# Start of a transformer block on one Trainium2 core: loads shared between two queues, x turned in pieces, sums joined at the end of a step

## The chip, the cores and the metric

The kernel runs on one core of a Trainium2 chip. The core has a matrix engine (PE, with its weight loads shown as PEld), a vector engine (DVE), a scalar engine (ACT), a general engine (POOL, also called GpSimd) and a queue engine that only starts transfers (SP). SP and POOL can both start DMAs; all of them run on the same 16 DMA engines. Each engine works through its own list in order, and waits on semaphores for the others. The metric is the device time of one execution in microseconds (us), as the median of several runs.

## What is computed

One transformer block on 512 tokens of width 2048: six modulation vectors from a conditioning vector c, a normed and modulated input h, a wide projection of h by `w_in`, a convolution mixer and a sparse attention mixer on the parts of the projection, an output projection, and a gated feed-forward network. The part that matters here is the beginning:

```python
sh_a, sc_a, g_a, sh_f, sc_f, g_f = jnp.split(jax.nn.silu(c) @ ada_w[l] + ada_b[l], 6, axis=-1)
h = modulate(rms_norm(x, norm_mix[l]), sh_a, sc_a)      # h * (1 + scale) + shift
proj = h @ w_in[l]
cb, cc, ch, q, kc, vc, ksl, vsl, kw, vw, gl = jnp.split(proj, splits, axis=-1)
...
```

All numbers are float32. x is 512 x 2048 (4.2 MB); the two modulation vectors that h needs take the first 4096 columns of `ada_w` (2048 rows each, 33.6 MB); three blocks of 512 columns of `w_in` are multiplied in this first stage (12.6 MB).

## The kernel before

The first stage runs from the start of the program to about 213 us; the rest of the block follows it with the matrix engine busy nearly all the time. The stage goes over the 2048 rows of `w_in` in eight **column steps** of 256 rows (two chunks of 128, `STEP` = 2). Before a column step can run, its 256 entries of shift and scale must be there, and each of them is a sum over all 2048 rows of `ada_w`. So there are also eight **sum steps** (`start_steps`), one for each column step. A sum step loads its 512 columns of `ada_w` as eight tiles of 512 KB, two transfers of 256 KB each. A tile holds two of the 16 row chunks. DVE multiplies each chunk by its entry of silu(c) and adds it to an accumulator `acc` (line 347 in the kernel before, 128 x 512 elements an instruction). From the second sum step on, the first four chunks are done by PE (`SHARE` = 4, line 341), and DVE's first instruction reads PE's result from PSUM as its addend. PE then adds up the 128 partitions (`column_sums`, line 224), and DVE makes the entries `mod` from it (lines 356 to 359).

x is loaded as four tiles of 1 MB; ACT squares and sums their halves (line 384), DVE scales the identity by the norms (`dg`, line 388), and PE turns and scales x in one product, 16 chunks times four tiles (line 413), which ACT copies to `xnT` (line 415).

A column step (`start_columns`) makes h of its two chunks on ACT from `xnT` and `mod`, split into a high part and a low part (lines 436, 439), then multiplies one block of `w_in` (`CKC`) into four PSUM tiles that stay open over all steps (lines 457 to 460), and, where a group of steps ends, blocks of two more column ranges (`CKS`, `CQ`) token by token (lines 115 to 117 through `mm3`), added to `ksv` and `q0` by DVE (line 495). Each block of `w_in` is also split into a high part on ACT (line 107) and a low part on DVE (line 109). float32 products are three such part products.

What sets the order: every engine's list is made once, when the program is built, from the order of the code and from explicit hints (`tc.issue_after(latest[...])`, not ahead of a noted instruction). `weave` lets the sum steps of later columns (the iterator `ahead`) run between the pieces of a column step, so many yields for each column step. All transfers of this stage are started by SP, in one list. A transfer also waits until the buffer that it writes is free: the `ada_w` tiles and the blocks of `CKS` and `CQ` share a ring of 8 buffers of 512 KB (`aring`), the blocks of `CKC` have a ring of 4 (`ring[0]`).

Of the kernel before, what the change touches and what calls it, by code (L numbers as in the profile page):

```python
# [72 lines left out]
def block_kernel(ctx: ExitStack, tc: tile.TileContext, a: dict, out: bass.AP):  # L73
# [83 lines left out]
    nc.scalar.activation(cT, cT, AF.Silu)  # L157
    xts = []
# [5 lines left out]

    const = cp.tile([P, CONST_W], F32, name="const")
    nc.sync.dma_start(const, a["shape_const"][:, :CONST_W])
    fold = sp.tile([P, 32], F32, name="fold")
    nc.sync.dma_start(fold, a["shape_const"][:, CONST_W:])
# [143 lines left out]
    aring = pool("araw", 8, stack=st0)  # L312
# [7 lines left out]
    def start_steps(k0):  # L320
# [6 lines left out]
        by_array = range(SHARE if k0 else 0)  # L327
        raws, pr = [], aux() if k0 else None
        for ka in range(0, KC, 2):
# [3 lines left out]
            for k in range(ka, ka + 2):  # L333
                w, s = raw[:, k - ka, :], cT[:, k:k + 1]
                if k in by_array:
# [3 lines left out]
                    with tc.issue_after(latest["columns"]):  # L339
                        for j, v in enumerate(raws):  # L340
                            nc.tensor.matmul(pr[32 * j:32 * j + 32, :], cz[:, k - 3 + j, :], v, start=k < 4,
                                             stop=k + 1 == SHARE, skip_group_check=True)
                    raws = []
                elif k == 0:
                    nc.vector.tensor_scalar(acc, w, s, None, op0=ALU.mult)
                else:
                    nc.vector.scalar_tensor_tensor(acc, w, s, pr if k == SHARE and k0 else acc, op0=ALU.mult, op1=ALU.add)
            yield
        if k0:
            yield  # L350
            yield
        with tc.issue_after(latest["columns"]):
# [6 lines left out]
        nc.vector.scalar_tensor_tensor(d[:, 1, :], d[:, 1, :], 1.0, g, op0=ALU.add, op1=ALU.mult)  # L359

# [4 lines left out]
    for name, n in ROWS.items():  # L365
        src = a[name].rearrange("l (k p) -> (l k) p", p=P) if name != "conv_w" else \
            a[name][0].rearrange("t (k p) -> (t k) p", p=P)
        nc.sync.dma_start(vrow[r0:r0 + n, :], src)
        at[name] = r0
        r0 += n  # L370
    nc.sync.dma_start(brow, a["ada_b"].rearrange("l (k p) -> (l k) p", p=P))
    for dst, src, n in ((cols, vrow, nrow), (bcol, brow, NB6)):
        ps = aux()
        nc.tensor.transpose(ps[:, :n], src, ident[:n, :n])
        nc.vector.tensor_copy(dst, ps[:, :n])

    dgs = []
    for i in range(NT):
# [3 lines left out]
        for m in range(2):  # L382
            junk = sp.tile([P, D // 2], F32, tag="junk", name="junk")
            nc.scalar.activation(junk, xt[:, m * D // 2:(m + 1) * D // 2], AF.Square, accum_out=sh[:, m:m + 1])
# [5 lines left out]
    for _ in range(4):  # L390
# [1183 lines left out]
```

## Time and profile before

| | us |
|---|---|
| runs of before: median (lowest to highest) | 2210.16 (2205.81 to 2211.21) |
| the profiled execution, whole | 2208.49 |
| its span in the trace | 2206.7 |
| PE busy in the span | 2141.2 (97%) |
| DVE busy | 1777.8 (81%) |
| ACT busy | 1077.9 (49%) |

The span leaves 1.8 us of the execution outside. The page's slices show where PE isn't full: the first two or three of 40 (each 55 us), and hardly anywhere else. DMA share, in the tables below, is the mean busy share of the 16 DMA engines, and the number behind it what they moved in GB/s. In the timeline a row has the start, the duration, the engine, the line and the operation, and in brackets how long the engine was idle before it and who ended that.

### The profile page before, as it was taken

The numbers are of one execution on the slowest core, as the hardware profiler recorded it, in microseconds if no ns is written. First come the engines' busy times: TensorE is split into PE (matmuls) and PEld (weight loads), VectorE is DVE, ScalarE is ACT, GpSimd is POOL, SyncE is SP. The second block draws the span as 40 slices with busy tenths as digits, with TensorE's granted clock in tenths as the row PEclk, the third lists the DMA queues.
The fourth block names the chain that finished last, engine by engine and source line by source line (L and its number), as shares of the span: only waits on it lengthen the run. The fifth ranks groups of instructions, "written<-read, shape, count | busy, mean of one in ns | idle before, by whom it ended". The sixth has DMA issues, their size and how long they took to land.

```text
span 2206.7 us, 30495 instructions
## 1 busy us (share of the span) xinstructions
PE 2141.2 (97%) x10981; PEld 1789.7 (81%) x10981; DVE 1777.8 (81%) x2762; ACT 1077.9 (49%) x1807; POOL 220.9 (10%) x284
## 2 busy tenths in 40 slices
PE   5899999999999898999999999999999999999998
PEld 4578778878878686888888888888888878888887
DVE  4787968878878697698888888888888876878787
ACT  5334434554543554745555555555554455545443
POOL 0000000000000223001110110100110021212132
PEclk9999999999999999999999999999999999999999
DMA  8993776545558978456666565666665499998897
GB/s 287 305 304 115 245 249 182 182 140 149 157 166 247 243 169 180 115 181 173 173 159 174 160 165 155 169 170 168 161 174 146 161 260 256 208 232 199 226 182 181
DMA packets 387932, 422.89 MB, mean 192 GB/s; under 512 B 21952, under 2 KB 293700, under 8 KB 387012
## 3 DMA queue, kind: packets, MB, share of 16 engines
q1 hardware_dynamic: 352388, 318.15, 46.2%
q0 software_dynamic: 35392, 102.79, 23.6%
q8 instruction: 86, 1.41, 0.3%
q14 instruction: 66, 0.54, 0.1%
HBM read 385.20 MB, written 19.94 MB: 184 GB/s over the span
## 4 chain that ended last, share of the span: by engine, by line
PE 88%; DMA 6%; DVE 2%; issue 1%; ACT 1%; POOL 1%; SPq 0%; ACTq 0%; POOLq 0%; DVEq 0%
PE main L1270 15%; PE aux L1270 11%; PE aux L1046 11%; PE main L1046 10%; PE main L1272 8%; PE aux L1272 6%; PE main L115 5%; PE main L117 5%; PE main L116 5%; DMA t<-in_w_out 2%; PE aux L861 2%; DMA y<-in_x 2%; PE aux L833 2%; PE aux L115 1%; PE aux L116 1%
## 5 line engine op out<-in xcount | busy, mean ns | idle before, releaser
L1270 PE MATMUL main<-hC,whi 128*128 128x512 f32 x1408 | 355.4, 394 | 0.0
L1270 PEld LDWEIGHTS main<-hC,whi 128*128 128x128 f32 x1408 | 253.8, 189 | 46.0 <-DVE hC L1137 0.5
L1270 PE MATMUL aux<-hC,whi 128*128 128x512 f32 x1072 | 268.8, 392 | 0.0
L1270 PEld LDWEIGHTS aux<-hC,whi 128*128 128x128 f32 x1072 | 192.8, 189 | 34.0
L1263 DVE TENSOR_TENSOR wlo<-xy,whi 128x1024 fp32r<-128x1024 f32 x135 | 164.6, 1219 | 62.6 <-ACT whi L1257 62.6
L1257 ACT CAST whi<-xy 128x1024 fp32r<-128x1024 f32 x135 | 141.4, 1048 | 147.2 <-PE main L1270 78.0
L1272 PEld LDWEIGHTS main<-hC,wlo 128*128 128x128 f32 x1408 | 192.3, 190 | 14.3
L1272 PE MATMUL main<-hC,wlo 128*128 128x256 f32 x1408 | 196.2, 282 | 0.0
L1046 PE MATMUL main<-wlo,phi 128*128 128x512 f32 x420 | 166.6, 398 | 13.1 <-DVE wlo L998 7.4
L1046 PE MATMUL aux<-wlo,phi 128*128 128x512 f32 x420 | 164.2, 391 | 1.8 <-DVE wlo L998 1.8
L1046 PE MATMUL main<-whi,phi 128*128 128x512 f32 x420 | 165.9, 395 | 0.0
L1046 PE MATMUL main<-whi,plo 128*128 128x512 f32 x420 | 165.7, 395 | 0.0
L1046 PE MATMUL aux<-whi,phi 128*128 128x512 f32 x420 | 163.5, 389 | 0.0
L1046 PE MATMUL aux<-whi,plo 128*128 128x512 f32 x420 | 163.5, 389 | 0.0
L115 PE MATMUL main<-alo,whi 128*128 128x512 f32 x384 | 155.7, 406 | 0.0
L1272 PEld LDWEIGHTS aux<-hC,wlo 128*128 128x128 f32 x1072 | 146.3, 190 | 10.5
L996 ACT CAST whi<-xy 128x1024 fp32r<-128x1024 f32 x88 | 92.8, 1055 | 120.3 <-PE main L1046 58.4
L117 PE MATMUL main<-ahi,whi 128*128 128x512 f32 x384 | 151.4, 395 | 0.0
L116 PE MATMUL main<-ahi,wlo 128*128 128x512 f32 x384 | 150.8, 393 | 0.0
L996 ACT CAST whi<-raw 128x1024 fp32r<-128x1024 f32 x90 | 94.9, 1055 | 113.8 <-PE aux L1046 57.7
L1272 PE MATMUL aux<-hC,wlo 128*128 128x256 f32 x1072 | 149.6, 282 | 0.0
L1257 ACT CAST whi<-t 128x1024 fp32r<-128x1024 f32 x84 | 88.2, 1050 | 120.7 <-PE aux L1270 64.8
(334 smaller groups left out, 4420.7 us busy)
## 6 DMA issues: line engine op xcount, KB each, us to landing
xy<-in_ffn_w SPq DMA_DIRECT2D x130, 512.0 KB, 4.8
raw<-in_ffn_w SPq DMA_DIRECT2D x112, 512.0 KB, 4.8
araw<-in_ada_w SPq DMA_DIRECT2D x208, 256.0 KB, 4.5
xy<-in_ffn_w POOLq DMA_DIRECT2D x66, 512.0 KB, 8.1
raw<-in_w_in SPq DMA_DIRECT2D x128, 192.0 KB, 3.5
xy<-in_ada_w SPq DMA_DIRECT2D x80, 256.0 KB, 3.7
graw<-in_ada_w SPq DMA_DIRECT2D x60, 256.0 KB, 2.8
acc<-graw POOLq DMA_DIRECT2D x60, 256.0 KB, 4.0
```

The costliest lines, as they stand in the source:

```text
L115: nc.tensor.matmul(ps, lhs[0], rhs[1], start=first, stop=False)
L116: nc.tensor.matmul(ps, lhs[1], rhs[0], start=False, stop=False)
L117: nc.tensor.matmul(ps, lhs[0], rhs[0], start=False, stop=last)
L833: nc.tensor.matmul(one[b], queries(g, i, h), kT[b][g][:, :L], start=True, stop=True)
L861: nc.tensor.matmul(po[:, b * HD:(b + 1) * HD], s["pT"][b][:, kb * P:(kb + 1) * P], vv[b][:, kb, g * HD:(g + 1) * HD], start=kb == 0, stop= ...
L996: nc.scalar.copy(hi, wt)
L1046: nc.tensor.matmul(ps, at_k[l][:, tok], wt[r][:, cs], start=begins and m == 0, stop=ends_ and j == i and m == 2, skip_group_check=True)
L1257: nc.scalar.copy(hi, t)
L1263: nc.vector.tensor_sub(lo, t, hi.bitcast(F32))
L1270: nc.tensor.matmul(ps, wt[0][:, ks[k]], hC[p][:, k, :], start=first and k == 0, stop=False, skip_group_check=True)
L1272: nc.tensor.matmul(ps[:, HS:], wt[1][:, ks[k]], hC[p][:, k, 0:HS], start=False, stop=last and k == HK - 1, skip_group_check=True)
```

## The change

**Who starts which transfer.** The table of constants, the small rows of gains and biases, the gate columns `wg` and every block of `w_in` behind the first column step are started by POOL in place of SP. `ada_w` stands directly behind x in SP's list. The first sum step loads six tiles, then the first block of `w_in`, then its last two tiles, then the two other first blocks. The ring `aring` has 10 buffers in place of 8.

**x is turned in pieces.** Two of the eight half tiles of x are squared by DVE in place of ACT. Six of the 16 chunks are turned first, tile by tile as the norms come; the other ten are written behind the first sums, and use PSUM tiles of both kinds.

**The array's share.** The first sum step too gives its first four chunks to PE; DVE starts its accumulator with chunk 4 and adds PE's result in one more instruction at the end of a step (line 351 of the changed kernel), in place of reading it in its first instruction. `weave` gives 12 yields to the first column step and 9 to each later one (before: 11, then 12 up to the seventh, then 2).

```diff
+    const = cp.tile([P, CONST_W], F32, name="const")
+    nc.gpsimd.dma_start(const, a["shape_const"][:, :CONST_W])
...
-    aring = pool("araw", 8, stack=st0)
+    aring = pool("araw", 10, stack=st0)
...
-        by_array = range(SHARE if k0 else 0)
-        raws, pr = [], aux() if k0 else None
+        by_array = range(SHARE)
+        raws, pr = [], None
...
-                elif k == 0:
+                elif k == SHARE:
                     nc.vector.tensor_scalar(acc, w, s, None, op0=ALU.mult)
                 else:
-                    nc.vector.scalar_tensor_tensor(acc, w, s, pr if k == SHARE and k0 else acc, op0=ALU.mult, op1=ALU.add)
+                    nc.vector.scalar_tensor_tensor(acc, w, s, acc, op0=ALU.mult, op1=ALU.add)
             yield
         if k0:
             yield
-            yield
-        with tc.issue_after(latest["columns"]):
+        nc.vector.tensor_add(acc, acc, pr)
+        with tc.issue_after(latest["columns"]) if k0 else nullcontext():
             ps = column_sums(aux, acc)
...
-        nc.sync.dma_start(vrow[r0:r0 + n, :], src)
+        nc.gpsimd.dma_start(vrow[r0:r0 + n, :], src)
...
+            if i * m % 2:
+                nc.vector.tensor_mul(junk, xh, xh)
+                nc.vector.reduce_sum(sh[:, m:m + 1], junk, axis=AX)
+            else:
+                nc.scalar.activation(junk, xh, AF.Square, accum_out=sh[:, m:m + 1])
...
-    for _ in range(4):
+    for _ in range(6):
         next(first)
...
-        if c0 == CKC:
-            return load(ring, rows(w_in, k, STEP, c0, n), STEP, n)
-        raw = aring.tile([P, 2, 512], F32, tag="araw", name="araw")
-        nc.sync.dma_start(raw, rows(w_in, k, STEP, c0, n))
+        raw = (ring[0] if c0 == CKC else aring).tile([P, 2, 512], F32, tag="raw" if c0 == CKC else "araw", name="raw")
+        with tc.issue_after(latest["block"]) if k else nullcontext():
+            (nc.gpsimd if k else nc.sync).dma_start(raw, rows(w_in, k, STEP, c0, n))
+        note("block")
...
+    def turn_x(ka, kb):
+
+        pst = [(aux, main)[(k - ka) % 2]() for k in range(ka, kb)]
+        for i in range(NT):
+            for k, ps in enumerate(pst, ka):
+                nc.tensor.matmul(ps[:, i * P:(i + 1) * P], xts[i][:, k * P:(k + 1) * P], dgs[i], start=True, stop=True)
+        for k, ps in enumerate(pst, ka):
+            nc.scalar.copy(xnT[k], ps)
+
+    turn_x(0, 6)
...
+        if k0 == 0:
+            with tc.issue_after(latest["block"]):
+                nc.gpsimd.dma_start(wg, rows(w_in, 0, KC, CGL, 32))
+            note("block")
+            turn_x(6, 12)
+            turn_x(12, KC)
+            ps_kv.extend(main() for _ in range(4))
+            gl_at[0] = aux()
...
-        n = 11 if k0 == 0 else 12 if k0 < 12 else 2
+        n = 12 if k0 == 0 else 9
```

What this makes of the lists, at three places. First SP's list at the start of the program, before: `xy` is a tile of x, `vrow` and `brow` the small rows, `araw` a buffer of the shared ring, `raw` one of the ring for `CKC`.

```order
L161 DMA xy<-in_x 128x2048 x4
L166 DMA const<-in_shape_const 128x704
L168 DMA fold<-in_shape_const 128x32
L368 DMA vrow<-in_norm_mix 16x128
L368 DMA vrow<-in_norm_ffn 16x128
L368 DMA vrow<-in_out_norm_conv 8x128
L368 DMA vrow<-in_conv_w 24x128
L368 DMA vrow<-in_out_norm_attn 8x128
L371 DMA brow<-in_ada_b 96x128
L332 DMA araw<-in_ada_w 128x2x256 x8
L96 DMA raw<-in_w_in 128x2x512
L399 DMA araw<-in_w_in 128x2x512 x2
```

The same list now, up to the first transfers of the stage behind, and POOL's list, whose place was empty of transfers before (five memsets stood there up to line 683):

```order
L165 DMA xy<-in_x 128x2048 x4
L331 DMA araw<-in_ada_w 128x2x256 x12
L399 DMA raw<-in_w_in 128x2x512
L331 DMA araw<-in_ada_w 128x2x256 x4
L399 DMA raw<-in_w_in 128x2x512 x2
L331 DMA araw<-in_ada_w 128x2x256 x110
L96 DMA raw<-in_w_in 128x2x512
```

```order
L159 DMA const<-in_shape_const 128x704
L161 DMA fold<-in_shape_const 128x32
L314 MEMSET cz 128x512
L369 DMA vrow<-in_norm_mix 16x128
L369 DMA vrow<-in_norm_ffn 16x128
L369 DMA vrow<-in_out_norm_conv 8x128
L369 DMA vrow<-in_conv_w 24x128
L369 DMA vrow<-in_out_norm_attn 8x128
L372 DMA brow<-in_ada_b 96x128
L456 DMA wg<-in_w_in 128x16x32
L399 DMA raw<-in_w_in 128x2x512 x21
L545 MEMSET v_1650 128x512
```

The small rows left the place between x and `ada_w`, and 21 blocks of `w_in` left SP's list, where they stood between the tiles of `ada_w`; 110 transfers of `ada_w` now follow each other there.

Second, PE's list around the first column sums (`acc_175`, now `acc_171`) and the first products of a column step, before:

```order
L413 MATMUL aux<-dg_140,xy 128x128
L413 MATMUL aux<-dg_151,xy 128x128
L413 MATMUL aux<-dg_162,xy 128x128
L413 MATMUL aux<-dg_173,xy 128x128
L224 MATMUL aux<-const,acc_175 128x128 x4
L459 MATMUL main<-ahi,wlo 128x512
L460 MATMUL main<-ahi,whi 128x512
```

and now:

```order
L415 MATMUL main<-dg_169,xy 128x128
L223 MATMUL aux<-const,acc_171 128x128 x4
L415 MATMUL aux<-dg_134,xy 128x128 x3
L415 MATMUL aux<-dg_146,xy 128x128 x3
L415 MATMUL aux<-dg_157,xy 128x128 x3
L415 MATMUL aux<-dg_169,xy 128x128 x3
L415 MATMUL aux<-dg_134,xy 128x128
```

Eleven more products of line 415 follow before the first one of a column step (line 482): of the 64 that turn x, 24 now stand behind the first column sums. ACT's list has the copies of all ten later chunks behind the first h.

Third, DVE's list around the second sum step (`acc_384`, now `acc_388`), before:

```order
L359 SCALAR_TENSOR_TENSOR mod<-mod,cols 128x2
L439 TENSOR_TENSOR alo<-h,ahi 128x512 x2
L347 SCALAR_TENSOR_TENSOR acc_384<-araw,cT,aux 128x512
L347 SCALAR_TENSOR_TENSOR acc_384<-araw,cT,acc_384 128x512 x9
L109 TENSOR_TENSOR wlo<-raw,whi 128x1024
L347 SCALAR_TENSOR_TENSOR acc_384<-araw,cT,acc_384 128x512 x2
L109 TENSOR_TENSOR wlo<-araw,whi 128x1024
L356 TENSOR_REDUCE mod<-aux 128x2x2
```

and now:

```order
L359 SCALAR_TENSOR_TENSOR mod<-mod,cols 128x2
L109 TENSOR_TENSOR wlo<-raw,whi 128x1024 x2
L452 TENSOR_TENSOR alo<-h,ahi 128x512
L345 TENSOR_SCALAR acc_388<-araw,cT 128x512
L452 TENSOR_TENSOR alo<-h,ahi 128x512
L347 SCALAR_TENSOR_TENSOR acc_388<-araw,cT,acc_388 128x512 x11
L351 TENSOR_TENSOR acc_388<-acc_388,aux 128x512
L109 TENSOR_TENSOR wlo<-raw,whi 128x1024
L345 TENSOR_SCALAR acc_503<-araw,cT 128x512
L347 SCALAR_TENSOR_TENSOR acc_503<-araw,cT,acc_503 128x512 x6
L356 TENSOR_REDUCE mod<-aux 128x2x2
```

The read of PE's share (`aux`) moved from the first instruction of the step to its own instruction at the end, and seven instructions of the third sum step now stand ahead of the `mod` of the second column step.

More of the change, by code (lines that the diff above doesn't have):

```diff
@@ L1 @@
 import itertools
-from contextlib import ExitStack
+from contextlib import ExitStack, nullcontext
 import numpy as np
@@ L157, in block_kernel @@
     nc.scalar.activation(cT, cT, AF.Silu)
+    const = cp.tile([P, CONST_W], F32, name="const")
+    nc.gpsimd.dma_start(const, a["shape_const"][:, :CONST_W])
+    fold = sp.tile([P, 32], F32, name="fold")
+    nc.gpsimd.dma_start(fold, a["shape_const"][:, CONST_W:])
     xts = []
@@ L359, in start_steps @@
         nc.vector.scalar_tensor_tensor(d[:, 1, :], d[:, 1, :], 1.0, g, op0=ALU.add, op1=ALU.mult)
+        note("mod")
     first = start_steps(0)
@@ L367, in block_kernel @@
             a[name][0].rearrange("t (k p) -> (t k) p", p=P)
-        nc.sync.dma_start(vrow[r0:r0 + n, :], src)
+        nc.gpsimd.dma_start(vrow[r0:r0 + n, :], src)
         at[name] = r0
         r0 += n
[L371 to L375, printed above, removed]
+    nc.gpsimd.dma_start(brow, a["ada_b"].rearrange("l (k p) -> (l k) p", p=P))
     dgs = []
@@ L394, in start_load @@
     def start_load(k, c0, n):
-        if c0 == CKC:
-            return load(ring, rows(w_in, k, STEP, c0, n), STEP, n)
-        raw = aring.tile([P, 2, 512], F32, tag="araw", name="araw")
-        nc.sync.dma_start(raw, rows(w_in, k, STEP, c0, n))
+        raw = (ring[0] if c0 == CKC else aring).tile([P, 2, 512], F32, tag="raw" if c0 == CKC else "araw", name="raw")
+        with tc.issue_after(latest["block"]) if k else nullcontext():
+            (nc.gpsimd if k else nc.sync).dma_start(raw, rows(w_in, k, STEP, c0, n))
+        note("block")
         return raw.rearrange("p k n -> p (k n)")
-    loaded = {c0: start_load(0, c0, 512) for c0 in (CKC, CKS, CQ)}
-    wg = sp.tile([P, KC, 32], F32, name="wg")
-    nc.sync.dma_start(wg, rows(w_in, 0, KC, CGL, 32))
+    loaded = {CKC: start_load(0, CKC, 512)}
     def start_split(k, c0, n):
         return load_split(ring, None, STEP, n, start_load(k, c0, n) if k else loaded[c0])
-    xnT = []
-    for k in range(KC):
-        ps = aux()
-        for i in range(NT):
-            nc.tensor.matmul(ps[:, i * P:(i + 1) * P], xts[i][:, k * P:(k + 1) * P], dgs[i], start=True, stop=True)
-        t = act.tile([P, S], F32, tag="alo", name="xnT")
-        nc.scalar.copy(t, ps)
-        xnT.append(t)
+    xnT = [act.tile([P, S], F32, tag="alo", name="xnT") for _ in range(KC)]
+    def turn_x(ka, kb):
[6 more added lines that the diff above has]
+    turn_x(0, 6)
+    for _ in range(2):
+        next(first)
+    loaded.update({c0: start_load(0, c0, 512) for c0 in (CKS, CQ)})
+    wg = sp.tile([P, KC, 32], F32, name="wg")
+    note("turned")
+    with tc.issue_after(latest["turned"]):
+        w0 = start_split(0, CKC, 512)
+    for dst, src, n in ((cols, vrow, nrow), (bcol, brow, NB6)):
+        ps = aux()
+        nc.tensor.transpose(ps[:, :n], src, ident[:n, :n])
+        nc.vector.tensor_copy(dst, ps[:, :n])
     note("columns")
@@ L422, in block_kernel @@
     hT, hF = [], []
-    ps_kv = [main() for _ in range(4)]
-    ps_gl = aux()
+    ps_kv, gl_at = [], {}
     for _ in first:
@@ L448, in split_next @@
             for c0, _, _, k, to in itertools.islice(later, 1):
-                to.append(start_split(k, c0, 512))
+                with tc.issue_after(latest["mod"]):
+                    to.append(start_split(k, c0, 512))
         for j in range(2):
```

20 lines of the change are left out of this document (9 added, 11 removed).

## The prediction

> **What bounds the kernel now.** I read the page's busy shares first (PE 97%: what is to be had lies where PE waits), then busy time by windows, to find where that is. Columns: window, length, busy time of PE, PEld, DVE, ACT and POOL with their counts, granted PE clock, DMA share, GB/s.
>
> ```profile
> PE 2141.2 (97%) x10981; PEld 1789.7 (81%) x10981; DVE 1777.8 (81%) x2762; ACT 1077.9 (49%) x1807; POOL 220.9 (10%) x284
> ...
> 2.60:20.00 17.40, 3.06 (x13) 2.80 (x14) 3.59 (x17) 11.59 (x22) 0.00 (x0) 1.00 0.86 330
> ...
> 60.00:140.00 80.00, 67.21 (x288) 46.22 (x287) 63.68 (x92) 23.77 (x29) 0.00 (x0) 0.94 0.92 299
> 140.00:172.00 32.00, 32.00 (x154) 23.74 (x154) 28.56 (x44) 9.86 (x12) 0.00 (x0) 1.00 1.00 331
> 172.00:214.00 42.00, 42.00 (x192) 33.73 (x192) 28.26 (x50) 19.05 (x34) 1.39 (x4) 1.00 0.18 52
> ```
>
> The change touches only the stage up to 213 us. There PE idles 12.8 us between 60 and 140, at a clock of 0.94, and is full from 140 on. The DMA engines are nearly full up to 172 and then almost empty. So the stage is short of data first and of PE time later, and PE ends it with some 40 us of work left over when the loads are done.
>
> Then the chain of waits, at the gap between the first and the second column step, and the start of PE's products (timeline: start, duration, what, idle before).
>
> ```profile
> 53.79 0.32 DVE acc L347
> 54.11 8.33 DMA araw<-in_w_in
> 62.52 1.06 ACT whi L107
> 63.60 1.23 DVE wlo L109
> 64.83 0.61 DVE mod L356
> 65.85 0.82 ACT ahi L436
> 66.72 0.50 PE main L459
> ...
> 39.92 1.09 PE L224 MATMUL aux<-const,acc 128*128 128x128 f32 x4 [4.94 <-DVE acc L347]
> 43.09 0.79 PE L459 MATMUL main<-ahi,wlo 128*128 128x512 f32 x1 [2.08 <-ACT ahi L436]
> ...
> 153.97 0.39 PE L459 MATMUL main<-ahi,wlo 128*128 128x512 f32 x1
> ...
> 190.14 0.39 PE L459 MATMUL main<-ahi,wlo 128*128 128x512 f32 x1
> ...
> 213.13 0.53 PE L509 MATMUL aux<-fold,gl 128*128 128x32 f32 x4
> ```
>
> A block of `w_in` is issued late (54.11), behind tiles of `ada_w` in SP's list, and DVE's low part of it stands ahead of the `mod` that PE waits for. Why SP was late is in its waits (who waited for whom, us, times, longest):
>
> ```profile
> SPq L332 <- DVE acc L347: 23.5, 24, 2.7
> SPq L332 <- PE aux L341: 18.3, 5, 7.1
> ```
>
> SP stood 41.8 us before full buffers, 18.3 of them for PE's share, and whatever was behind in its list stood too. This is what the change can take away.
>
> **The start.** The chain's row for x, SP's own rows, and groups and rows of what the first products wait for (groups: line, engine, shapes, count, then busy us and mean ns of one):
>
> ```profile
> 2.60 11.17 DMA xy<-in_x
> ...
> 6.39 0.32 SPq L368 DMA_DIRECT2D vrow<-in_out_norm_conv  x1
> ...
> 13.79 0.32 SPq L371 DMA_DIRECT2D brow<-in_ada_b  x1
> 14.69 3.98 SPq L332 DMA_DIRECT2D araw<-in_ada_w  x8
> ...
> L347 DVE SCALAR_TENSOR_TENSOR acc<-araw,cT,acc 128x512 f32<-128x512 f32 x92 | 68.9, 748 | 3.0 <-DMA araw<-in_ada_w 1.1
> ...
> L495 DVE TENSOR_TENSOR xy<-aux,xy 128x512 f32<-128x512 f32 x32 | 21.8, 686 | 7.3 <-PE aux L117 7.1
> ...
> L109 DVE TENSOR_TENSOR wlo<-raw,whi 128x1024 fp32r<-128x1024 f32 x10 | 12.2, 1221 | 3.1 <-ACT whi L107 3.1
> ...
> L356 DVE TENSOR_REDUCE mod<-aux 128x4 f32<-128x512 f32 x8 | 5.5, 689 | 5.5 <-PE aux L224 5.5
> ...
> 26.09 0.58 ACT L415 COPY xnT<-aux 128x512 f32<-128x512 f32 x1 [0.31 <-PE aux L413]
> 26.98 0.58 ACT L415 COPY xnT<-aux 128x512 f32<-128x512 f32 x1 [0.31 <-PE aux L413]
> ...
> 28.41 1.07 ACT L415 COPY xnT<-aux 128x512 f32<-128x512 f32 x2
> ...
> 42.23 1.52 ACT L436 ACTIVATE ahi<-xnT,mod 128x512 fp32r<-128x512 f32 x2 [6.62 <-DVE mod L359]
> ...
> 43.65 1.50 ACT L436 ACTIVATE h<-xnT,mod 128x512 f32<-128x512 f32 x2
> ```
>
> The small rows kept SP from `ada_w` until 14.69, though x had landed by 13.77 (2.60 and 11.17); in the window 2.6 to 20 the engines were 0.86 full. That hole of 2.4 us closes. Until the last tile of the first sum step there now lie x (11.2 us in before), 4.2 MB of `ada_w` and one block (0.5 MB) on SP, and 1.2 MB on POOL (constants, small rows, `wg`, and a block whose buffer is free at once). At the prices per MB below this is 11.2 + 4.7 x 3.09 + 1.2 x 5.0 = 31.7, so the last tile lands near 34.5. Behind it two chunks on DVE (1.5), the new addition (an addition from PSUM of 128x512 takes 0.69), column sums (1.1), the reduction (0.69) and two small instructions: `mod` at 38.9 against 42.1. But the gain of 3.2 is given back: 24 of the 64 products that turn x now stand between, 5.4 us at before's pace (a chunk, which is four such products, per 0.9 us: 26.09 to 26.98), and ACT copies ten chunks (0.54 us each, two in 1.07) behind the first h (2.9 us for four). The four open PSUM tiles come free with the fourth, sixth, eighth and tenth copy, so products start at 44.3 and the last group at 47.5. The first token products stand at 51.3 where they stood at 51.74. **Term: -0.5 us**, between -3 (if the copies hide) and +2 (if they don't overlap at all).
>
> DVE takes two half squares off ACT, each a product of 128x1024 like a `wlo` (1.22 us) and a reduction, estimated at 1.1 to 1.4; DVE is busy for 3.59 of 17.4 us there, so this costs nothing. If POOL's small rows are late, the transposes that read them stand in PE's list ahead of the later turns; they have until about 22 us.
>
> **The price of POOL's queue.** All transfers run on the same 16 engines; what a byte costs by queue is read where one queue is alone, and where both run (queue, packets, MB, share of the engines): SP alone over 20 to 170 us, POOL alone over 804 to 836, both over 1796 to 1806.
>
> ```profile
> q1 hardware_dynamic: 42216, 45.25, 93.2%
> ...
> q0 software_dynamic: 1990, 6.62, 106.9%
> ...
> q0 software_dynamic: 333, 1.23, 61.8%
> q1 hardware_dynamic: 340, 1.72, 43.6%
> ```
>
> SP's loads take 0.932 x 150 / 45.25 = 3.09 us of all engines per MB, POOL's 1.069 x 32 / 6.62 = 5.17, beside SP's 5.0. The shares add up to 1.05 where both run, so the times add with about 5% of overlap. 21 blocks of 0.52 MB, `wg` and the small things are 11.7 MB (x, `ada_w` and three blocks, 39.3 MB, stay on SP): **their move costs 11.7 x 1.9 = 22 us of engine time**. A column step now takes 4.19 x 3.09 + 1.57 x 5.0 = 20.8, with overlap 19.8, where it took 17.8. That is the main charge against the change. Its bounds: nothing, if POOL's packets only fill holes, and 22 us if nothing overlaps.
>
> [...]
>
> **The later steps.** Counted from 0, column steps 0 and 1 start their products at 43.09 and 66.72 in before (above), step 5 at 153.97 and step 7 at 190.14, and these last ones run at PE's pace of 18.1 us. With two queues, SP runs ahead through `ada_w` as far as 10 buffers reach, one whole step of eight tiles and two blocks, and a block goes out when its own buffer is free. DVE no longer begins a step by waiting for PE:
>
> ```profile
> 50.63 0.75 DVE L347 SCALAR_TENSOR_TENSOR acc<-araw,cT,aux 128x512 f32<-128x512 f32 x1 [4.76 <-PE aux L341]
> ...
> L347 DVE SCALAR_TENSOR_TENSOR acc<-araw,cT,aux 128x512 f32<-128x512 f32 x7 | 5.2, 745 | 7.7 <-PE aux L341 7.2 <-DMA araw<-in_ada_w 0.4
> ```
>
> That removes 7.2 us of waits and adds seven additions of 0.69 (4.8 us): DVE's load per step rises to about 18.5 us (12 of 0.75, five additions of 0.69, two `alo` of about as much, three `wlo` of 1.22, and 1.0 for `mod`), still under the DMA's 19.8. Step 1 doesn't gain: its `mod` now stands behind seven instructions of the next sum step, whose sixth tile (two for PE, four for DVE) lands near 34.5 + 3.2 (two blocks) + 13.0 (eight tiles) + 9.7 (six tiles) + 5.2 (two blocks of POOL) = 65.6, so products start at 67, as before (66.72). From there each step takes the DMA's 19.8 us, and at the end the lead of `ada_w` is used up: its last tiles come 0.65 of a step (8 us) early, so step 7 needs only the blocks. It starts at 67 + 6 x 19.8 - 8 = 178. Friction of 0.7 us a step, from DVE and PE taking turns, makes it 182, against 190.14. PE's own pace allows 175 (six steps of 18.1). Behind it lie 23 us of products in both (190.14 to 213.13). **Term: -8 us**, between -15 (PE's pace) and +7 (22 us of engine time unhidden, less the 15).
>
> The sum: the profiled execution of 2208.49 (span 2206.7 and 1.8 around it) less 8 to 8.5 is 2200; the median of the runs is 1.7 above that execution, so I say **2201**. The end of the stage moves through unchanged: behind 214 PE is full.
>
> **Rivals.** First, **PE alone bounds the stage**: blocks always come in time. For it: a round of blocks takes only 8 us of 20. It would be so if POOL's bytes cost what SP's do. [...] Step 7 at 175: -15, 2194. Against it: DMA engine time of 180 us in all. Second, **a wash**: the price of POOL's bytes eats the saved waits (no overlap, 20.8 a step and friction): step 7 at 67 + 6 x 21.5 - 8 = 188, -2, 2207. Third, on the other side, **the DMA engines become the bound with before's holes**: their time of 39.3 x 3.09 + 11.7 x 5.0 = 180 us at before's share of 0.92 ends at 198; a step takes 22.6, step 7 starts at 67 + 6 x 22.6 - 8 = 195, +5, 2214. It decides once the share stays under 0.96. [...] What the trace has on POOL's issues beside a busy DVE (a window, and one issue in it):
>
> ```profile
> 1800.00:1840.00 40.00, 40.00 (x178) 33.15 (x177) 27.61 (x41) 23.81 (x38) 13.72 (x16) 1.00 1.06 223
> ...
> 1811.57 0.86 POOL L1004 DMA_DIRECT2D xy<-in_ffn_w  x1 [1.86 <-DVE wlo L998]
> ```
>
> [...]
>
> **How the numbers follow.** Forecast (2196 to 2205) 0.48; PE's pace 0.12; a wash 0.22; DMA bound 0.13; POOL held up 0.05. Range 2189 to 2216: from PE's pace, a few us under, to the third rival. A measurement can tell 0.3% (6.6 us, so below 2203.5 or above 2216.8). Faster: 0.12 and four fifths of 0.48, with a little of the wash: 0.52. Slower: the two last: 0.18. Same: 0.30.
>
> **What would show it.** Right: no hole in the DMA share from 2.6 to 170 us; 3 us of engine time per MB on SP's queue and 5 on POOL's; `mod` of the first step near 39 but first token products still near 51; PE idle between 60 and 140 down from 12.8 to some 6; last column step near 182; DVE's waits for line 341 gone. Wrong: DMA full at under 290 GB/s to beyond 185 with PE waiting for ACT's h (third rival), issues of POOL longer than 0.9 us (fourth), or PE without a gap from 51 on (first). It also fails if a wait moves behind the stage, since I took everything behind 214 us as shifted whole.

## The result, and the profile after

The changed kernel takes **2186.71 us** (median of 4 runs, 2186.07 to 2190.16) against 2210.19 for the kernel before (4 runs; the 2210.16 of the table ahead is the lower of the two middle ones): a ratio of 0.9901, 95% interval 0.9884 to 0.9918, or -23.5 us. The forecast was 2201 with a range of 2189 to 2216: the sign was right, the size was not, and the time lies outside the range. The profiled execution took 2186.07 us, with a span of 2184.3. A second set of runs of the same kernel (after_again) gave a median of 2186.95 and a ratio of 0.9903 (0.9890 to 0.9917); two of its seven executions took over 4300 us, the profiled one among them, so its trace says nothing about the start.

Busy time by windows of the changed kernel (columns as in the prediction):

```profile
2.60:20.00 17.40, 5.70 (x28) 4.56 (x28) 7.20 (x17) 9.38 (x18) 5.40 (x9) 0.98 0.99 376
...
60.00:140.00 80.00, 79.22 (x374) 57.45 (x377) 72.81 (x113) 27.91 (x34) 10.66 (x15) 1.00 1.04 341
140.00:172.00 32.00, 31.82 (x150) 24.51 (x146) 23.50 (x36) 11.80 (x14) 2.66 (x4) 1.00 0.45 161
```

PE's idle time between 60 and 140 fell from 12.8 us to 0.8, its granted clock there rose from 0.94 to 1.00, and the loads run at 341 GB/s where they ran at 299, so that after 140 the DMA engines are only 0.45 full. Rows of the changed kernel's timeline (start, duration, what): the last part of the first `mod`, the first products, the first token products, column steps 1 and 7, and the first product on `fold`, with which the stage ends (called the fold below):

```profile
38.44 0.16 DVE L359 SCALAR_TENSOR_TENSOR mod<-mod,cols 128x2 f32<-128x2 f32 x1
...
43.96 0.48 PE L482 MATMUL main<-ahi,wlo 128*128 128x512 f32 x1
...
50.76 0.39 PE L115 MATMUL aux<-wlo,ahi 128*128 128x512 f32 x1
...
63.34 0.39 PE L482 MATMUL main<-ahi,wlo 128*128 128x512 f32 x1
...
170.83 0.39 PE L482 MATMUL main<-ahi,wlo 128*128 128x512 f32 x1
...
193.82 0.53 PE L532 MATMUL aux<-fold,gl 128*128 128x32 f32 x4
```

The first three stand near where the forecast had them (38.9, 44.3, 51.3). Step 1 starts at 63.34 where 67 was forecast, step 7 at 170.83 where 182 was. The fold moved from 213.1 to 193.8, which is 19.3 of the 22.4 us that the two spans differ by. The rest is no more than these parts differ between runs: span less fold is 1993.6 before, 1990.5 after, and between 1989.7 and 1995.2 in the runs below, plain_later apart (1981.6), which changes the stage behind.

What SP waited for between 14 and 180 us, and the queues from 20 to 150 us (packets, MB, share of the engines), both of the changed kernel:

```profile
SPq L331 <- DMA araw<-in_ada_w: 23.6, 54, 2.2
SPq L331 <- DVE acc L347: 20.7, 20, 3.0
...
SPq L331 <- PE aux L341: 2.8, 3, 2.0
```

```profile
q1 hardware_dynamic: 34914, 34.96, 83.1%
q0 software_dynamic: 2801, 10.23, 21.7%
```

SP's 18.3 us before PE's share are down to 2.8. But POOL's queue cost 0.217 x 130 / 10.23 = 2.76 us of all engines' time per MB, not 5.0, beside SP's 3.09.

### The profile page after: what moved, and what is told of

It reads as the page before. It is cut to its first block, busy times and chain, and to the rows that moved or that the text cites. A ratio compares the mean times of both kernels' runs of the same rounds, so it can differ in the third digit from the quotient of the medians.

```text
span 2184.3 us, 30547 instructions
## 1 busy us (share of the span) xinstructions
PE 2135.7 (98%) x10989; PEld 1785.3 (82%) x10989; DVE 1780.6 (82%) x2770; ACT 1076.4 (49%) x1803; POOL 241.8 (11%) x314
## 4 chain that ended last, share of the span: by engine, by line
PE 86%; DMA 7%; DVE 3%; issue 2%; ACT 1%; POOL 1%; SPq 0%; DVEq 0%; ACTq 0%; POOLq 0%
PE main L1293 15%; PE aux L1293 11%; PE aux L1069 11%; PE main L1069 10%; PE main L1295 8%; PE aux L1295 6%; PE main L117 5%; PE main L115 5%; PE main L116 5%; DMA araw<-in_ada_w 3%; PE aux L884 2%; PE aux L856 2%; DMA t<-in_w_out 1%; DMA y<-in_x 1%; DVE acc L347 1%
```

## The experiments

All runs in one table. Columns: start of the first products, of step 1 and step 7, and the fold, from each run's timeline; pieces, in how many places of PE's list the 16 gate products (`wg`) stand; median of the runs and the ratio to before with its interval. The ratio is to runs of before that were made beside each (medians 2207.4 to 2210.2). The starts come from one profiled execution of each run; plain_later, whose first stage is the changed kernel's, has its fold 1.8 us later, so a difference of 1 or 2 us at the fold says little by itself.

| run | first | step 1 | step 7 | fold | pieces | us | ratio |
|---|---|---|---|---|---|---|---|
| before | 43.1 | 66.7 | 190.1 | 213.1 | 6 | 2210.19 | 1 |
| changed | 44.0 | 63.3 | 170.8 | 193.8 | 4 | 2186.71 | 0.9901 (0.9884-0.9918) |
| one_list | 41.7 | 61.1 | 167.7 | 190.7 | 5 | 2184.46 | 0.9885 (0.9870-0.9900) |
| pool_only | 47.4 | 70.6 | 194.8 | 217.8 | 5 | 2212.05 | 1.0015 (1.0006-1.0025) |
| sum_blocks | 47.0 | 66.5 | 192.9 | 215.9 | 4 | 2208.25 | 0.9994 (0.9984-1.0003) |
| plain_later | 44.0 | 63.3 | 172.6 | 195.6 | 4 | 2178.98 | one run |
| ring8 | 44.0 | 64.0 | 170.1 | 193.1 | 4 | 2186.34 | 0.9899 (0.9882-0.9915) |
| old_join | 42.3 | 62.8 | 175.5 | 198.5 | 7 | 2194.22 | 0.9940 (0.9925-0.9954) |
| old_pace | 42.4 | 64.1 | 175.4 | 198.4 | 6 | 2192.08 | 0.9930 (0.9915-0.9944) |
| old_both | 42.4 | 61.6 | 190.3 | 213.3 | 7 | 2210.13 | 1.0011 (1.0001-1.0021) |
| join_only | 43.3 | 65.6 | 189.3 | 212.3 | 8 | 2206.79 | 0.9995 (0.9986-1.0004) |
| pace_only | 43.4 | 65.1 | 176.9 | 199.9 | 6 | 2193.26 | 0.9938 (0.9923-0.9953) |
| join_pace | 43.2 | 65.9 | 176.0 | 199.0 | 8 | 2193.90 | 0.9942 (0.9927-0.9957) |
| join_pace_glue | 43.0 | 64.5 | 172.3 | 195.2 | 4 | 2190.17 | 0.9918 (0.9900-0.9936) |
| old_join_glue | 42.4 | 62.8 | 177.4 | 200.4 | 4 | 2193.74 | 0.9936 (0.9920-0.9952) |
| one_glue | 41.2 | 60.6 | 166.6 | 189.6 | 4 | 2183.64 | 0.9892 (0.9876-0.9907) |
| turn_early | 38.5 | 60.4 | 175.6 | 198.5 | 8 | 2192.66 | 0.9937 (0.9922-0.9952) |
| early_glue | 38.0 | 60.8 | 170.3 | 193.3 | 4 | 2188.42 | 0.9914 (0.9896-0.9932) |
| glue_small_sp | 47.5 | 66.8 | 172.9 | 195.9 | 4 | 2189.38 | 0.9909 (0.9895-0.9922) |

### Is it the second list?

one_list: the changed kernel, later blocks issued by SP again.

```diff
-            (nc.gpsimd if k else nc.sync).dma_start(raw, rows(w_in, k, STEP, c0, n))
+            nc.sync.dma_start(raw, rows(w_in, k, STEP, c0, n))
```

> The changed kernel, with the later w_in blocks issued by SP again, between the ada_w tiles; buffers, join, start and pace as changed. Theory A (the blocks' own list is the main gain): SP's waits for full buffers hold up the blocks again, PE idles 6 to 12 us between 60 and 140, the last column step starts at 182 to 190 instead of 171, the stage's last products (the fold) stand at 205 to 212 instead of 193.8, and the run takes 2198 to 2206 us. Theory B (the join at the end and ten buffers are the main gain, the list is not): the fold stays within 192 to 197 and the run within 2184 to 2191.

pool_only: the kernel before, with this edit alone (the same for the blocks of `CKC`).

```diff
-        nc.sync.dma_start(raw, rows(w_in, k, STEP, c0, n))
+        (nc.gpsimd if k else nc.sync).dma_start(raw, rows(w_in, k, STEP, c0, n))
```

> The kernel before, with one edit: the w_in blocks of the later column steps are issued by POOL. Start, join, eight buffers and pace as before. Theory A (the blocks' own list is the main gain): the step between the first two column steps shrinks by 2 us or more, the fold stands at 195 to 203 instead of 213.1, and the run takes 2190 to 2200. Theory B (join and buffers): the fold stands at 208 to 214, and the run takes 2204 to 2212.

Theory A, which was also the forecast's reason, falls from both sides. With one list the fold stands at 190.7, ahead of the changed kernel's; with the list alone it stands at 217.8, behind before's. Of these 4.7 us 4.3 are lost ahead of the first products (47.4 against 43.1): POOL starts three later blocks at 1.3 us, beside x, and PE gets its small rows at 19.8 instead of 16.1. From the first products to the fold both kernels take 170 us, so the list brings nothing there either. A window of one_list, then what SP (14 to 180 us) and PE (43 to 200) waited for in pool_only:

```profile
60.00:140.00 80.00, 80.00 (x374) 58.37 (x373) 74.46 (x111) 27.38 (x33) 0.00 (x0) 1.00 0.99 329
```

```profile
SPq L332 <- DVE acc L347: 31.8, 30, 3.4
SPq L332 <- PE aux L341: 21.4, 7, 6.6
...
PE aux L224 <- DVE acc L347: 15.2, 5, 7.4
```

On one list PE has no idle time at all from 60 to 140. In pool_only SP runs ahead into full buffers and stands there for longer than in before (18.3 and 23.5 there): with the blocks gone from its list, the tiles still wait for PE and DVE.

### Where did the price of 5 us per MB come from?

sum_blocks gives the blocks the kind of transfer that the forecast's price was read from: in 804 to 836 us all of POOL's loads add to what lies in the buffer (`accum_op`).

```diff
-            (nc.gpsimd if k else nc.sync).dma_start(raw, rows(w_in, k, STEP, c0, n))
+            if k:
+                nc.gpsimd.memset(raw, 0.0)
+                nc.gpsimd.dma_start(raw, rows(w_in, k, STEP, c0, n), accum_op=ALU.add)
+            else:
+                nc.sync.dma_start(raw, rows(w_in, k, STEP, c0, n))
```

> The changed kernel, with each later block set to zero by POOL and then loaded by a DMA that adds to what is there, as the loads of 804 to 836 us do from which the forecast took its price. Theory A (the price of 5 us of engine time per MB belongs to adding DMAs, and with it the forecast's sum would have come true): POOL's queue takes 4.5 to 5.2 us per MB here, a column step 19 to 20, the fold stands at 201 to 206 and the run takes 2196 to 2201. Theory B (the price belongs to the other stage's matrix or moment): POOL's queue stays under 3.3 us per MB, the fold at 193 to 197, 2185 to 2191. Theory C (the price is as forecast, but PE hides it): 4.5 us per MB or more, and still the fold at 193 to 197.

plain_later does the reverse where the price was read; it leaves out the sums that these loads form:

```diff
-                nc.gpsimd.dma_start(wt, block(*more_), accum_op=ALU.add)
+                nc.gpsimd.dma_start(wt, block(*more_))
```

> The changed kernel, with the adding DMAs of the w_out and ffn_w products (line 1027) made plain loads; this leaves out the sums of blocks that they form. Theory A (adding is what costs 5 us per MB): POOL's queue, alone in a window of the w_out stage, takes 2.5 to 3.3 us of all engines' time per MB instead of 5.2. Theory B (it is the matrix, its rows of another pitch, or the queue): 4.5 to 5.2 as before. The time gets 0 to 10 us shorter by A, behind the stage at the start, where PE idles 5 us near 700 to 740.

Queues of sum_blocks from 20 to 150 us, with its window; then of the changed kernel and of plain_later from 780 to 800 us:

```profile
q1 hardware_dynamic: 31658, 31.30, 75.3%
q0 software_dynamic: 3805, 7.34, 30.9%
```

```profile
60.00:140.00 80.00, 70.07 (x311) 49.44 (x310) 60.29 (x93) 24.93 (x32) 24.16 (x23) 0.96 1.06 290
```

```profile
q0 software_dynamic: 1415, 4.12, 107.6%
```

```profile
q0 software_dynamic: 1432, 4.87, 73.0%
```

Adding blocks cost 0.309 x 130 / 7.34 = 5.47 us per MB; the loads of the later stage cost 1.076 x 20 / 4.12 = 5.22 when they add and 0.73 x 20 / 4.87 = 3.00 when they don't. Theory A holds for the price: it belongs to the adding, not to POOL's queue. It does not hold for the sum: with the price made true a column step takes (192.9 - 66.5) / 6 = 21.1 us and the fold stands at 215.9, where 201 to 206 was expected. The engines are full (1.06) at 290 GB/s and PE idles 9.9 us. By its step and its 2208 us this is the forecast's second rival (21.5 a step, 2207), not its forecast. The mean hides one long step: step 4 takes 30.4 us (124.5 to 154.9), the others 17 to 21, and the chain of waits through it is loads of `ada_w`. (Part of it may be the wait for POOL's clearing, which wasn't run apart.) plain_later was also 7.7 us shorter than the changed kernel, in one run; its gain lies behind the stage, where PE is full from 700 to 740 (it idles 5.1 us there in the changed kernel).

### Buffers, join and pace

ring8 has 8 buffers in place of 10, old_join and old_pace each undo one edit of the changed kernel, and join_only and pace_only make one edit of the kernel before.

```diff
-    aring = pool("araw", 10, stack=st0)
+    aring = pool("araw", 8, stack=st0)
```

> The changed kernel with 8 buffers for tiles of ada_w and blocks instead of 10. Theory D (the two buffers are the main gain): the fold stands at 203 or later and the run takes 2196 us or more. Theories C and E (join, pace): the fold at 193 to 198, 2185 to 2191.

```diff
-                elif k == SHARE:
+                elif k == SHARE and not k0:
...
-                    nc.vector.scalar_tensor_tensor(acc, w, s, acc, op0=ALU.mult, op1=ALU.add)
+                    nc.vector.scalar_tensor_tensor(acc, w, s, pr if k == SHARE else acc, op0=ALU.mult, op1=ALU.add)
...
-        nc.vector.tensor_add(acc, acc, pr)
+        else:
+            nc.vector.tensor_add(acc, acc, pr)
```

> The changed kernel with the old join in the steps after the first: DVE's first product of a sum step reads PE's share out of PSUM again, and the addition at the end goes. Queues, ten buffers, start and pace as changed. Theory C (the join is the main gain: with it DVE and the buffers no longer wait for PE): the fold stands at 203 to 212, PE idles 6 us or more between 60 and 140, SP waits 10 us or more for PE's share, and the run takes 2196 to 2206 us. Theory E (the pace of nine pieces of sums for each column step is the main gain): the fold at 193 to 198 and 2185 to 2191.

```diff
-        n = 12 if k0 == 0 else 9
+        n = 11 if k0 == 0 else 12 if k0 < 12 else 2
```

> The changed kernel with the pace of before: 11 pieces of sums beside the first column step, 12 beside the next ones, instead of 12 and then 9. Theory E (the pace is the main gain: sums run ahead of the column step that needs its blocks now, and DVE and the loads are spent on tiles that aren't needed yet): the fold stands at 203 to 212, PE idles 6 us or more between 43 and 140, and the run takes 2196 to 2206 us. Theory C (the join): the fold at 193 to 198, 2185 to 2191.

join_only, made on the kernel before:

```diff
-                elif k == 0:
+                elif k == (SHARE if k0 else 0):
...
-                    nc.vector.scalar_tensor_tensor(acc, w, s, pr if k == SHARE and k0 else acc, op0=ALU.mult, op1=ALU.add)
+                    nc.vector.scalar_tensor_tensor(acc, w, s, acc, op0=ALU.mult, op1=ALU.add)
...
-            yield
+            nc.vector.tensor_add(acc, acc, pr)
```

> The kernel before, with one edit: PE's share of a sum step is added at its end, and DVE starts with a plain product; everything on SP, eight buffers, start and pace as before. Theory C (the join): the fold stands at 198 to 205 instead of 213.1, and the run takes 2192 to 2200 us. Theory E (the pace): 208 to 214, 2204 to 2212.

```diff
-        n = 11 if k0 == 0 else 12 if k0 < 12 else 2
+        n = 13 if k0 == 0 else 10
```

> The kernel before, with the pace alone: a sum step has ten pieces there, and 13 stand beside the first column step and 10 beside each later one. Theory G: DVE and the buffers still wait for PE's share, so the fold stands at 206 to 213 and the run takes 2200 to 2209 us. The rival (the pace does it alone): the fold at 203 or before, 2198 or less.

The buffers are worth nothing (theory D falls). The join alone brings 0.8 us at the fold and no time that can be measured. **The pace alone moves the fold by 13.2 us**; theory G expected 7 at most from it, and its rival was right. Undone in the changed kernel, the join and the pace cost 4.7 and 4.6 us at the fold. Theories C and E had 9 us or more for one of the two and at most 4 for the other, so neither holds there. What PE waited for from 43 to 200 us, in before and in pace_only:

```profile
PE aux L224 <- DVE acc L347: 8.7, 3, 3.5
PE main L459 <- ACT ahi L436: 5.3, 2, 3.3
PE aux L115 <- DVE wlo L109: 0.8, 1, 0.8
```

```profile
PE main L459 <- ACT ahi L436: 2.1, 1, 2.1
PE aux L224 <- DVE acc L347: 2.0, 2, 1.5
PE aux L115 <- DVE wlo L109: 1.3, 2, 1.0
```

The column sums (line 224) stand in PE's list at the place that the weave gives them, and PE takes its list in order: in before it stood 3.45 us ahead of the sums at 101.52. Their places beside the products of the same step, in before (steps 3 and 6) and in pace_only (step 3):

```profile
101.52 0.66 PE L224 MATMUL aux<-const,acc 128*128 128x128 f32 x4 [3.45 <-DVE acc L347]
113.00 0.39 PE L459 MATMUL main<-ahi,wlo 128*128 128x512 f32 x1
...
157.60 0.60 PE L224 MATMUL aux<-const,acc 128*128 128x128 f32 x4
...
173.19 0.39 PE L459 MATMUL main<-ahi,wlo 128*128 128x512 f32 x1
```

```profile
93.79 0.60 PE L224 MATMUL aux<-const,acc 128*128 128x128 f32 x4
...
100.94 0.39 PE L459 MATMUL main<-ahi,wlo 128*128 128x512 f32 x1
```

In before 12 pieces of sums stand beside each column step from the second to the sixth, though a sum step has ten, and two beside each of the last two. So the sums run ahead: 11.5 us before the products that need them at step 3, 15.6 at step 6, where 7.2 is enough in pace_only. In the middle of the stage PE stands for sums that nobody needs yet, and SP's list is full of their tiles; at the end (172 to 214) DVE is busy for 28.3 of 42 us and the DMA engines for 0.18, while PE has its work left over. The window of pace_only shows it, with the same queue, buffers and bytes as before (there PE 67.21, clock 0.94, share 0.92):

```profile
60.00:140.00 80.00, 77.45 (x363) 55.81 (x362) 72.04 (x105) 29.65 (x37) 0.00 (x0) 1.00 0.98 321
```

And SP's waits for PE's share in pace_only (14 to 180 us), which were 18.3 us in before:

```profile
SPq L332 <- PE aux L341: 28.2, 7, 7.9
```

They grew, and PE hardly idles: a queue that waits for buffers is no sign by itself that it is late.

### Join and pace together

join_pace makes both edits on the kernel before; old_both undoes both in the changed kernel.

> The kernel before, with two edits: PE's share added at the end of a sum step, and the pace of 12 pieces beside the first column step and 9 beside each later one. One list on SP, eight buffers, start and turns as before. Theory G (join and pace together are the gain of the later steps; either alone leaves the other's wait, so that the join alone brought nothing): the fold stands at 196 to 203 instead of 213.1, PE idles under 4 us between 60 and 140, and the run takes 2191 to 2199 us. Theory H (without the start of the changed kernel the blocks still come late): the fold at 206 to 213 and 2200 to 2209.

> The changed kernel with the old join and the old pace at once; queues, ten buffers and start as changed. Undone singly they cost 4.6 and 4.7 us at the fold. If the two add, it stands at 203 and the run takes 2196 us. By theory G they stand for all but 1 to 3 us (the start) of the gain, so the fold is at 209 to 213 and the run takes 2203 to 2208. If they hide each other: 198 and 2192.

On the kernel before, the join adds 0.9 us at the fold to the pace, which is within the spread, and no time. In the changed kernel it counts: undone with the new pace it costs 4.7 us, with the old pace 14.9 (198.4 to 213.3). With both undone, everything else of the change (second list, ten buffers, start, turns) is worth nothing: 1.0011 of before. What the old join brings back in the changed kernel is mostly one wait, of DVE in step 1 (timeline of old_join):

```profile
47.79 0.75 DVE L347 SCALAR_TENSOR_TENSOR acc<-araw,cT,aux 128x512 f32<-128x512 f32 x1 [7.05 <-PE aux L341]
```

In before it is 4.76 us at 50.63 (the row in the prediction). The changed kernel puts turns and products ahead of PE's share there, so that the old join waits longer; that the new start needs the new join is read from this wait and not from a run of its own.

### A piece that nobody edited

join_pace is still 8.3 us behind one_list at the fold. One difference isn't in the diff: the four gate products of a round write 32 output rows each, and in join_pace they stand in eight pieces, in the changed kernel in four. PE's timeline of join_pace and of the changed kernel (two records for each product):

```profile
64.89 1.05 PE L468 MATMUL aux<-h,wg 128*32 128x512 f32 x2
71.53 1.06 PE L468 MATMUL aux<-h,wg 128*32 128x512 f32 x6
88.32 1.05 PE L468 MATMUL aux<-h,wg 128*32 128x512 f32 x4
```

```profile
68.87 1.07 PE L491 MATMUL aux<-h,wg 128*32 128x512 f32 x8
```

One product takes 1.05 us, and four that stand together 1.07. The three glue runs hold them together:

```diff
         if k0 + n in (4, 8, 12, 16):
-            for j in range(4):
+            with tc.issue_after(latest["columns"]):
+                for j in range(4):
...
```

> join_pace, with the four products of the gates (32 output columns each, line 468) of a round held together in PE's list behind the column step's last product. They stand in eight pieces in join_pace and in four in the changed kernel; a piece of four took 1.0 us there and pieces of one to three 0.9 each here. Theory I (a piece costs the same however few products it has): the fold stands at 194.7 to 196 instead of 199.0, and the run takes 2189 to 2191 us; the 1 to 5 us that are then left to the changed kernel belong to the start. The rival (PE only waits elsewhere instead, or the pieces hide idle time): the fold at 198 to 200.

> old_join, with the gates' products held together in the same way (seven pieces become four). If the 4.7 us that the old join cost at the fold were mostly the three pieces more: the fold at 195 to 196.3 instead of 198.5, the run at 2189 to 2191. If they are DVE's and SP's waits for PE's share: the fold stays at 197.5 to 199, the run at 2192 to 2195.

> one_list (which has five pieces) with the gates' products held together. By theory I one piece less: the fold at 189.5 to 190.2 instead of 190.7, the run at 2182.5 to 2184.5. If POOL's list is worth something after all and one_list was a lucky order, it comes out at the changed kernel's 2186 to 2188.

join_pace gains 3.8 us at the fold and 3.7 in the run for four pieces (join_pace_glue): theory I holds there. one_list gains 1.1 for one (one_glue), within the spread, and 0.5 of it lies ahead of the first products. old_join_glue shows the limit. Three pieces less, and the run takes as long as before (2193.74 against 2194.22) with a fold 1.9 us later, and PE's waits for the sums are up from 4.4 to 7.8 us: the time saved on PE turned into waiting. So the 4.7 us of old_join are not its pieces; the wait of 7.05 us above is the longest that it has and the changed kernel hasn't. one_glue is as fast as one_list, so that one list was no lucky order; the two lie 2 to 3 us below the changed kernel, with intervals that overlap.

### The start

turn_early is one_list with the last ten chunks of x turned ahead of the first column sums; early_glue is that with the gate products together.

```diff
+    turn_x(6, 12)
+    turn_x(12, KC)
     for _ in first:
         pass
...
-            turn_x(6, 12)
-            turn_x(12, KC)
```

> One list (the run one_list) with one more edit: the last ten chunks of x are turned ahead of the first column sums, where PE stands 6.6 us, and no longer behind them. Theory F (from its first product on, PE alone bounds the stage, so what the first product gains the stage gains): the first product stands at 36.5 to 38.5 instead of 41.7, the fold at 186 to 188 instead of 190.7, and the run takes 2179 to 2182 us. The rival (ACT's copies of the turned chunks or its h, or the loads, are as late as PE): the first product at 40 or later, or PE idles again before 140, the fold at 189 to 192 and 2183 to 2187.

> turn_early (eight pieces) with the gates' products held together. By theory I four pieces less: the fold at 194 to 195.5 instead of 198.5, the run at 2188 to 2190, still behind one_list, because the sums of the second and third step stay late for it (DVE's part). If the scattered pieces were a sign of the new order and it falls back to that of one_list with an earlier first product: the fold at 186 to 189 and 2179 to 2183.

Theory F falls. The first product came 3.2 us earlier, as meant, and step 1 didn't (60.8 in early_glue, 60.6 in one_glue), because its `mod` is made when it was. The reductions of step 1 in DVE's timeline of one_glue and of early_glue:

```profile
56.78 0.69 DVE L356 TENSOR_REDUCE mod<-aux 128x4 f32<-128x512 f32 x1 [0.28 <-PE aux L223]
```

```profile
56.43 0.69 DVE L356 TENSOR_REDUCE mod<-aux 128x4 f32<-128x512 f32 x1 [5.78 <-PE aux L223]
```

In early_glue DVE stood 5.78 us for the column sums, in PE's list, and lost that for the next sum step: step 2 starts at 77.1 instead of 74.4. (Its next reduction is at 73.3 instead of 70.8.) The four pieces less were worth 5.2 us of the 7.8 by which turn_early lay behind one_list.

glue_small_sp is one_glue with `const`, `fold`, `vrow` and `brow` on SP again, ahead of `ada_w`.

> one_glue with the constants and the small rows issued by SP again, in before's places around x (const and fold ahead of x, the rows behind it), so that ada_w starts some 11 us later in SP's list. Theory J (the start's gain is the hole that the small rows left in the DMA engines behind x, 2.4 us in before): the DMA share in the window 2.6 to 20 falls from 1.00 to 0.85 to 0.9, the first column sums and the first products come 1.5 to 3 us later (products at 43 to 44.2 instead of 41.2), the fold stands at 191 to 193 instead of 189.6 and the run takes 2185 to 2188. The rival (DVE's sums bound step 1 anyway, as in early_glue, where a first product 3 us earlier left step 1 at 60.8): the fold stays at 189 to 190.5.

It cost 6.3 us at the fold, more than either theory had. Windows of glue_small_sp, and its longest wait of DVE there (1.6 in one_glue):

```profile
2.60:20.00 17.40, 4.94 (x24) 4.58 (x24) 6.66 (x15) 9.17 (x18) 0.07 (x1) 1.00 0.94 345
20.00:43.00 23.00, 15.17 (x85) 11.84 (x86) 14.01 (x23) 7.73 (x13) 0.00 (x0) 0.74 1.08 358
```

```profile
DVE cols L430 <- PE aux L429: 5.1, 1, 5.1
```

The hole in the DMA engines is only 1 us (0.94 of 17.4). The tiles come late, PE's clock falls to 0.74 (0.85 in one_glue), and DVE stands behind the copy of `cols`, whose transposes wait in PE's list.

> The changed kernel unchanged, in the same call as one_glue's variant, to see how much of the 3 to 4 us between its fold (193.8) and that of one_list and one_glue (190.7 and 189.6) is its own spread. In its first profile PE waited 1.6 us for a tile at 17.4 and then ran its turns at half pace to 23 (granted clock 0.80 in 20 to 43, 0.85 in one_list), so its first product came at 44.0. If that is chance, the first product comes at 42.3 to 42.5 as in old_pace and old_join, whose start is the same, the fold at 191.5 to 192.5 and the run at 2184.5 to 2186; if it belongs to the kernel (POOL's early block beside the tiles), they stay at 44, 193.8 and 2186 to 2188.

after_again gave no start to compare (see the result); its time shows that 2187 is the kernel's own. ring8 and plain_later, which start as the changed kernel does, give the start: PE waits 1.71 and 1.68 us at the same place there, its granted clock is 0.55 from 19.0 to 22.8 as in the changed kernel, and the first products stand at 44.0. So the slow start isn't chance. It is 1.6 of the 2.3 us by which one_list's first products are ahead (old_pace, which keeps POOL's list and the clock, has them at 42.4). Why the tile comes later in these three programs isn't shown, and whether POOL's list costs the rest stays open.

## Why the prediction went wrong

**The start** came out by its numbers: `mod` at 38.4 (38.9), first products at 44.0 (44.3), token products at 50.8 (51.3; before's stood at 51.97, and the sum's 51.74 is the load of their weights), the hole behind x gone (share 0.99). Its path was another, so part of this is luck. The forecast let the last tile decide, at 5.0 us per MB for POOL's bytes. In the trace DVE works without a stop from 26.57 up to the new addition, behind a wait for PE's transpose of the small rows:

```profile
26.57 0.23 DVE L430 COPY cols<-aux 128x72 f32<-128x72 f32 x1 [3.25 <-PE aux L429]
...
35.63 0.69 DVE L351 TENSOR_TENSOR acc<-acc,aux 128x512 f32<-128x512 f32 x1
```

And PE had run slowly just ahead of these transposes (the last section). In the four runs with the same start in which it didn't (old_pace, old_join, old_both, old_join_glue), the first products stand at 42.4.

**The price of POOL's queue** is the first step that failed: "their move costs 11.7 x 1.9 = 22 us of engine time". The 5.0 to 5.17 us per MB were read in windows where POOL's loads add. Line 1004 of the code says so, and I read only the queue. Plain bytes cost 2.76 here; by the same sum a step of loads then takes 4.19 x 3.09 + 1.57 x 2.76 = 17.3, less than PE's 18.1. The price carried the whole step of 19.8 us, and through the four blocks ahead of it also "step 1 doesn't gain": 63.3, not 67 (sum_blocks, where the price holds, has 66.5).

**The pace** is the second: the sum has no term for it. I explained PE's idle time by SP's waits for full buffers, and so by the list, the join and the buffers. Of these, the list brings nothing by itself, nor do the buffers, nor does the join on the kernel before, while the pace alone brings 13.2 of the 19.3 us. The waits of SP, on which the argument rested, cost nothing by themselves (28.2 us of them in pace_only).

**PE's pace**, the first rival, at 0.12, is what came: the steps take (170.8 - 63.3) / 6 = 17.9 us (18.1 assumed), and PE's gaps from 60 on sum to 1.0 us. It gave 2194: its step 7 at 175 is 4.2 us late, 3.7 of them because it kept step 1 at 67, and the stage behind, which the change leaves alone, took 3.1 us less in the profiled execution.

**The ledger** at the fold: 213.1, less 13.2 for the pace, 0.9 for the join beside it (within the spread), 3.8 for gate products that the list's new order puts together (shown by join_pace_glue), and 5.6 for the start, turns and buffers (one_glue against join_pace_glue), makes 189.6; the changed kernel is 4.2 behind that, 2.8 of it ahead of the first product. Of these 2.8, PE's slow stretch is 1.6: see below. Another order of the edits would share the gain otherwise, as old_join and old_both show.

**POOL held up**, the rival at 0.05, didn't come, and no run shows it: POOL's 21 issues of blocks took 0.71 to 0.73 us each in the changed kernel. One of them, in the window in which DVE is 0.91 busy:

```profile
61.46 0.72 POOL L399 DMA_DIRECT2D raw<-in_w_in  x1 [13.28 <-DMA araw<-in_ada_w]
```

The 0.72 us are no more than the 0.73 of the first block at 9.58. In before the issue in the prediction's row (1811.57), in a window in which DVE was busy for 27.6 of 40 us, took 0.86 us.

## What to carry to other kernels

Before a price is taken from another stage, look at what kind of transfer it is there, not only at its queue (on POOL's queue 5.22 us per MB when it adds, 3.00 when it doesn't). When a queue waits for buffers, ask first whether anybody needs what it loads yet: a side job woven in faster than its user consumes it costs the main engine time in the middle that it can't give back at the end. And test each edit alone on the old kernel and undone on the new one, since here the two gave different answers for the join.

## What the runs showed of the hardware

- A DMA that adds cost 5.22 (changed kernel, 780 to 800) to 5.47 us (sum_blocks, 20 to 150) of all engines' time per MB, a plain one on the same queue 2.76 (changed kernel, 20 to 150) to 3.00 (plain_later, 780 to 800).
- One product of 32 output rows took as long as four together (1.05 us in join_pace, 1.07 in the changed kernel).
- Behind a wait of 1.64 us PE ran at a granted clock of 0.55 for some 3.7 us (19.07 to 22.8, changed kernel). The start of the changed kernel and of old_pace, which has the same list there:

```profile
19.07 1.85 PE L341 MATMUL aux<-araw,cz 128*32 128x512 f32 x4 [1.64 <-DMA araw<-in_ada_w]
20.85 1.98 PE L415 MATMUL aux<-dg,xy 128*128 128x128 f32 x8
```

```profile
19.11 1.05 PE L341 MATMUL aux<-araw,cz 128*32 128x512 f32 x4 [0.78 <-DMA araw<-in_ada_w]
20.09 1.16 PE L415 MATMUL aux<-dg,xy 128*128 128x128 f32 x8
```

Behind 1.64 us of waiting the same products took 1.7 times as long as behind 0.78, the granted clock from 19.0 to 22.8 was 0.55 instead of 1.00, and the first products came at 44.0 instead of 42.4. At this place waits of 1.64 to 1.71 us (the changed kernel, ring8, plain_later) were followed by such a stretch, and just ahead of it one of 2.22 in glue_small_sp (0.54 from 20.59 to 24.3); waits of 0.78 to 1.29 (old_pace, old_join, old_both, old_join_glue) were not. The length alone doesn't decide: in before a gap of 3.45 us ahead of 101.5 was followed by 3.7 us at 0.59, one of 3.02 ahead of 83.6 by none (1.00 from 83.6 to 87.3). What decides it is not shown. In before the clock of 0.94 between 60 and 140 took, by an estimate, about 4 us (0.06 of the 67.2 us in which PE was busy) beside the 12.8 us of gaps.
